# A head's query norms made chunk by chunk between the chunks of the next column block, in a linear-attention layer

## The chip, the cores and the metric

The kernel runs on one core of a Trainium2 chip. The core has five engines that run side by side, each through its own queue in order: TensorE (PE; its weight loads are shown as PEld), VectorE (DVE), ScalarE (ACT), GpSimd (POOL) and SyncE (SP), which here starts the transfers. The metric is device time in microseconds (us), the median of several runs.

## The reference, cut to what matters

The trunk has two layers over 1024 tokens behind 16 learned meta tokens, 1040 rows of width 1024, in float32. Layer A is gated DeltaNet attention with eight heads of width 128; then come a shared latent key/value set and layer B, a latent attention. The change is in layer A, where each head's queries are normalised:

```
z = h @ w_in                                        # 1040 x 4112
qkv = silu(causal_dwconv(z[..., :3072], conv_w))    # 4 taps
q, k, v = ...                                       # eight heads of 128 each
q = l2_norm(q) * (DN_DK ** -0.5)                    # x * rsqrt(sum(x*x) + EPS)
k = l2_norm(k)
...
o = gated_delta_rule(q, k, v, g, beta)              # chunkwise recurrence
o = rms_norm(o, o_gain) * silu(gate)
```

A scale on a query row only scales the output row, which is normalised again. So the kernel leaves the queries as they are and puts the sum of their squares into the epsilon of the output's norm: with s the sum of squares of a query row, the tile `epsq` holds EPS * P * s + EPS * EPS * P, and it is read once, after the last head.

## The kernel before, in words

Layer A keeps the normed input transposed in SBUF, as a high and a low part (`hT_hi`, `hT_lo`), 128 features by 1040 tokens for each of eight feature tiles. A **column block** is 128 columns of the input weight: one head's keys, values, queries or gate. `conv_acts` makes one block in three token chunks, `TOKC = [(0, 272), (272, 656), (656, 1040)]`. For each chunk `gemm_T` issues 24 matmuls on PE (eight feature tiles, three products of high and low parts, L91 to L93) into one of two "mm" banks of PSUM. ACT copies the bank to `z` (L370), POOL makes the first tap (L372), DVE the other three (L375), and ACT applies SiLU in place (shown as L82, the line of the helper `act`).

Heads go in pairs. For a pair h0, h1 the program text says: values of h0, their rows turned by PE (`natural`, L497 and L502), values of h1, queries of h0, rows of h1's values, queries of h1, `query_prep(h0)`, keys of the next pair's first head, `finish_inverses`, `query_prep(h1)`, keys of the next pair's second head, then the recurrence of both heads, step by step (`scan_tile`, L611 to L625), and the preparation of the next pair's keys. The last pair has no next keys; behind it in the text stand the gate blocks.

`query_prep` first makes the norms. ACT squares the three chunks of the head's queries `qT` into the tile `sq`. PE multiplies each of nine token tiles of `sq` (the meta tokens and eight of 128) with a column of ones, so that the sums over the 128 features fall one token to a partition (L475; a float32 matmul shows as two records, so a head has 18). DVE turns the nine columns into `epsq` with two instructions (L477). Then PE multiplies keys by queries for eight tiles (L483, 16 records) and the meta tokens (L487), and DVE multiplies by the decay (L484, L488). PSUM tiles with the tag "tr" (norms, turned rows, key by query products and more) share three banks. `sq` has the tag "vT", and with it the one buffer in which a head's values stand between `conv_acts` and `natural`.

What each engine does when is drawn up when the kernel is built: an instruction is placed on its engine's queue when, by the plan, what it needs is there, and among those that could go the earlier one in the text goes first. At run time each queue is then strictly followed, and semaphores make it wait.

Of the kernel before, what the change touches and what calls it, by code (L numbers as in the profile page):

```python
# [16 lines left out]
F32 = mybir.dt.float32  # L17
F32R = mybir.dt.float32r
BF16 = mybir.dt.bfloat16
AF = mybir.ActivationFunctionType  # L20
ALU = mybir.AluOpType
PSUM = bass.MemoryType.PSUM

P = 128
D = 1024
NM = 16
T = 1024
L = NM + T
NT = T // P
# [3 lines left out]
EPS = 1e-6  # L33
# [7 lines left out]
TOKC = [(0, 272), (272, 656), (656, 1040)]  # L41


def tok(t):

    return (0, NM) if t < 0 else (NM + P * t, NM + P * (t + 1))
# [70 lines left out]
def body(ctx: ExitStack, tc: tile.TileContext, I, out):  # L117
    nc = tc.nc
    V, A, G, TE, SY = nc.vector, nc.scalar, nc.gpsimd, nc.tensor, nc.sync
    tpool, nm, act, mm3, split_w, split_ps = tools(tc)  # L120
# [31 lines left out]
    one = ones[:, 0:1]  # L152
# [5 lines left out]
    def col(key, k=0):  # L158
        c = off[key] + k
        return pcol[:, c:c + 1]  # L160
# [21 lines left out]
    with ExitStack() as la:  # L182
# [5 lines left out]
        def bank(tag, shape):  # L188
            return pp.tile(shape, F32, tag=tag, name=nm(tag), bufs={'mm': 2, 'tr': 3, 'fin': 1, 'ch': 2}[tag])
# [17 lines left out]
        def gemm_T(hi, lo, c, m=P, tag="mm"):  # L207
            a, b = TOKC[c]
            ps = bank(tag, [P, 512])[0:m, 0:b - a]
            for kt in range(KT):  # L210
                mm3(ps, hi[:, kt, :], lo[:, kt, :], hT_hi[:, kt, a:b], hT_lo[:, kt, a:b],
                    kt == 0, kt == KT - 1)
            return ps

        with ExitStack() as l0:
# [9 lines left out]
            n = 0  # L225
# [15 lines left out]
            for c, (a, b) in enumerate(TOKC):  # L241
                tiles = [t for t in range(-1, NT) if a <= tok(t)[0] < b]
                xss = []
                for t in tiles:
# [8 lines left out]
                                    op0=ALU.mult, op1=ALU.mult)  # L253
                    xss.append((xs, r0, k))
                for kt in range(KT):
                    ps = bank("tr", [P, 512])
# [4 lines left out]
        with ExitStack() as l0:  # L261
# [8 lines left out]
            for c, (a, b) in enumerate(TOKC):  # L270
                ps = bank("fin", [P, 512])[0:4 * H, 0:b - a]
# [7 lines left out]
            ps = bank("tr", [P, 512])  # L279
            for t in range(-1, NT):  # L280
                a, b = tok(t)
                s = t if t >= 0 else NT
# [12 lines left out]
            def ntile(name, w=NT + 1):  # L295
                pool = cp if name in ("oss", "epsq", "ro", "half", "y2") else na
                return pool.tile([P, w, H], F32, tag=name, name=name)

            oss, ro = ntile("oss"), ntile("ro")
            beta, g, egc, ekd, necb, egl, epsq, nbeta = (ntile(x) for x in (  # L300
                "beta", "g", "egc", "ekd", "necb", "egl", "epsq", "nbeta"))
# [20 lines left out]
            ps = bank("tr", [P, 512])  # L322
# [17 lines left out]
        kp = ld.enter_context(tpool(name="kA", bufs=2))  # L340
# [13 lines left out]
        def weights(c0):  # L354

            n = order.index(c0)
            for c in order[n:n + 2]:
                if c not in ready:
                    ready[c] = load_w(c)
            return ready.pop(c0)  # L360

        def conv_acts(c0, tag, bufs):

            hi, lo = weights(c0)
            m = c0 // P
            z = zp.tile([P, 3 + L], F32, tag="z", name=nm("z"))
            y = kp.tile([P, L], F32, tag=tag, name=nm(tag), bufs=bufs)
            G.memset(z[:, 0:3], 0.0)
            for c, (a, b) in enumerate(TOKC):
                A.copy(z[:, 3 + a:3 + b], gemm_T(hi, lo, c))  # L370
                yc = y[:, a:b]
                G.tensor_scalar(out=yc, in0=z[:, a:b], scalar1=col("cw", m), scalar2=1.0,  # L372
                                op0=ALU.mult, op1=ALU.mult)
                for j in range(1, 4):
                    V.scalar_tensor_tensor(out=yc, in0=z[:, a + j:b + j], scalar=col("cw", 24 * j + m), in1=yc,  # L375
                                           op0=ALU.mult, op1=ALU.add)
                act(yc, yc, AF.Silu)
            return y

        def halves():  # L380
            return [(hf, slice(4 * hf, 4 * hf + 4)) for hf in range(2)]
# [83 lines left out]
        def query_prep(h, c):  # L465

            qT, kn, att, attm = c["qT"], c["kn"], c["att"], c["attm"]
            sq = kp.tile([P, L], F32, tag="vT", name=nm("sq"), bufs=1)
            ps = bank("tr", [P, 512])
            for a, b in TOKC:  # L470
                act(sq[:, a:b], qT[:, a:b], AF.Square)
            for t in range(-1, NT):
                a, b = tok(t)
                s = t if t >= 0 else NT
                TE.matmul(ps[0:b - a, s:s + 1], sq[:, a:b], one, start=True, stop=True)  # L475
            for rows, s in ((slice(0, P), slice(0, NT)), (slice(0, NM), slice(NT, NT + 1))):
                V.tensor_scalar(out=epsq[rows, s, h:h + 1].rearrange("p t o -> p (t o)"), in0=ps[rows, s],  # L477
                                scalar1=EPS * P, scalar2=EPS * EPS * P, op0=ALU.mult, op1=ALU.add)
            for half, s4 in halves():
                ps = bank("tr", [P, 512])  # L480
                for j in range(4):
                    a, b = tok(4 * half + j)
                    TE.matmul(ps[:, P * j:P * j + P], kn[:, a:b], qT[:, a:b], start=True, stop=True)  # L483
                V.tensor_tensor(out=att[half], in0=ps.rearrange("p (t i) -> p t i", i=P),  # L484
                                in1=att[half], op=ALU.mult)
            ps = bank("tr", [P, 512])
            TE.matmul(ps[:NM, 0:NM], kn[:, 0:NM], qT[:, 0:NM], start=True, stop=True)  # L487
            V.tensor_tensor(out=attm, in0=ps[:NM, 0:NM], in1=attm, op=ALU.mult)  # L488
# [103 lines left out]
        def scan_meta(h, c):  # L592
            ps = bank("ch", [P, 512])
            u = sp.tile([NM, P], F32, tag="um", name=nm("um"))
            TE.matmul(ps[:NM, 0:P], c["Nm"], c["vbm"], start=True, stop=True)
            A.copy(u, ps[:NM, 0:P])
            TE.matmul(ps[:, P:2 * P], c["kdm"], u, start=True, stop=True)
            S = sp.tile([P, P], F32, tag=f"S{h % 2}", name=nm("S"))
            V.tensor_copy(S, ps[:, P:2 * P])
            TE.matmul(ps[:NM, 2 * P:3 * P], c["attm"], u, start=True, stop=True)  # L600
            o = sp.tile([P, P], F32, tag="o", name=nm("o"), bufs=3)
            j = sp.tile([P, P], BF16, tag="js", name=nm("junk"), bufs=1)
            A.copy(o[:NM], ps[:NM, 2 * P:3 * P])
            act(j[:NM], o[:NM], AF.Square, accum_out=oss[:NM, NT, h:h + 1])
            SY.dma_start(o_scr[0:NM, h * P:(h + 1) * P], o[:NM])
            return S
# [26 lines left out]

        hs = {h: {} for h in range(H)}

        def keys_of(h):
            hs[h]["kn"] = conv_acts(D + h * P, "kn", 4)

        def values_of(h):
            hs[h]["vT"] = conv_acts(2 * D + h * P, "vT", 1)  # L640

        def queries_of(h):
            hs[h]["qT"] = conv_acts(h * P, "qT", 2)

        def value_rows(h):
            hs[h]["vb"], hs[h]["vbm"] = natural(hs[h]["vT"], beta, h, "vb")

        def prepare(h0):
            U = kp.tile([P, 2, NT, P], F32, tag="U", name=nm("U"), bufs=2)
            for h in (h0, h0 + 1):  # L650
                hs[h].update(key_prep(h, hs[h]["kn"], U[:, h - h0]))
            hs[h0]["Us"] = U
            invert_blocks((h0 // 2) % 2, h0)

        keys_of(0)
        keys_of(1)
        prepare(0)
        for h0 in range(0, H, 2):
            h1, more = h0 + 1, h0 + 2 < H
            values_of(h0)  # L660
            value_rows(h0)
            values_of(h1)
            queries_of(h0)
            value_rows(h1)
            queries_of(h1)
            query_prep(h0, hs[h0])
            if more:
                keys_of(h0 + 2)
            finish_inverses(h0, hs[h0]["Us"])
            query_prep(h1, hs[h1])  # L670
            if more:
                keys_of(h1 + 2)
            Ss = {h: scan_meta(h, hs[h]) for h in (h0, h1)}
            for t in range(NT):
                for h in (h0, h1):
                    Ss[h] = scan_tile(h, t, hs[h], Ss[h])
            if more:
                prepare(h0 + 2)
# [27 lines left out]
        norms = output_norms()  # L706
# [61 lines left out]
    def bank2(tag, shape):  # L768
        tag = {"mm": "sc", "tr": "bd", "tb": "pt"}.get(tag, tag)
        return ps_b.tile(shape, F32, tag=tag, name=nm(tag), bufs={"sc": 5, "bd": 2, "pt": 1}[tag])  # L770

    with ExitStack() as lb:
# [204 lines left out]
        with ExitStack() as lg:  # L977
            wg = lg.enter_context(tpool(name="wg", bufs=2))
            for h in range(H):
                hi, lo = wg0 if h == 0 else load_wg(wg, h)  # L980
                z = wg.tile([P, T], F32, tag="z", name=nm("z"))
                for half in range(2):
                    c = slice(512 * half, 512 * half + 512)
                    cc = slice(NM + 512 * half, NM + 512 * half + 512)
                    ps = bank2("mm", [P, 512])
# [484 lines left out]
```

## Time and profile before

| | |
|---|---|
| median of three runs | 1351.07 us |
| lowest and highest of them | 1346.55 and 1354.87 us |
| the profiled execution's own time | 1351.8 us |
| its span, from the first to the last instruction | 1350.1 us |
| granted TensorE clock, mean over the span | 0.989 |
| layer A's pairs, from the first query blocks to the last pair's recurrence | about 98 to 545 us of the span |

Times in the profile are counted from the span's start. A row of the chain of waits or of the timeline gives start, length, engine, line, operation, "out<-in" in the program's names, shapes and a count; idle time before an instruction stands in square brackets with what ended it. "tr", "mm" and so on are the tags of PSUM tiles. A row of windows gives the stretch, its width, then for each engine its busy time and instructions in brackets, then the mean granted share of the TensorE clock, the DMA engines' busy share and their GB/s.

### The profile page before, as it was taken

Reading aid. Unit: us, or ns where it says so; the run is one execution under the profiler, and the core shown is the slowest. Engines: PE = TensorE matmul, PEld = TensorE weight load, DVE = VectorE, ACT = ScalarE, POOL = GpSimd, SP = SyncE. Lnnn points to the kernel's source line nnn. Section 1 sums busy time; section 2 is a strip of 40 time slices with the busy share of each in tenths; the row PEclk is TensorE's granted clock in tenths of the full one; section 3 lists DMA queues with packets and bytes.
Section 4 is the critical chain, followed back from the end, with each engine's and each line's share of the span. In section 5 each row is a group of like instructions: output and inputs, shape, how many; then the busy total and the mean of one; then the engine's idle time right before and its main releaser. Section 6 shows DMA issues by size and latency. Waiting matters only on the chain.

```text
span 1350.1 us, 24895 instructions
## 1 busy us (share of the span) xinstructions
PE 1306.3 (97%) x9064; PEld 1181.7 (88%) x9064; DVE 900.1 (67%) x2601; ACT 534.8 (40%) x1694; POOL 412.8 (31%) x680
## 2 busy tenths in 40 slices
PE   6999999999999999999999999998999999998998
PEld 4879989989998999997888798887999999998876
DVE  6669879968978884633553765224888878788221
ACT  6442343244325322211222243116777677776100
POOL 3344224323421320060101402212535435347000
PEclk9999999999999999999999999999999999999999
DMA  6111202111211113255441302311111101014443
GB/s 185 41 25 48 56 20 62 40 42 37 59 49 32 50 32 96 72 159 178 145 147 68 95 1 84 121 47 57 44 38 35 56 21 36 21 36 149 133 124 125
DMA packets 116924, 96.81 MB, mean 72 GB/s; under 512 B 28462, under 2 KB 106094, under 8 KB 116802
## 3 DMA queue, kind: packets, MB, share of 16 engines
q1 hardware_dynamic: 116802, 95.23, 23.7%
q8 instruction: 71, 1.16, 0.4%
q14 instruction: 51, 0.42, 0.1%
HBM read 68.19 MB, written 27.01 MB: 71 GB/s over the span
## 4 chain that ended last, share of the span: by engine, by line
PE 75%; DVE 8%; DMA 5%; POOL 5%; ACT 4%; issue 3%; SPq 0%; DVEq 0%; ACTq 0%; POOLq 0%
PE mm L91 7%; PE mm L93 7%; PE mm L92 7%; PE sc L93 6%; PE sc L92 6%; PE sc L91 6%; PE bd L91 3%; PE bd L93 3%; PE bd L92 3%; PE pt L1312 2%; PE tr L483 1%; DMA raw<-in_a_w_out 1%; ACT junk L82 1%; DMA out<-raw 1%; PE ch L625 1%
## 5 line engine op out<-in xcount | busy, mean ns | idle before, releaser
L91 PE MATMUL mm<-hT_hi,whi 128*128 128x384 f32 (+1 forms) x768 | 256.8, 334 | 3.5 <-DVE whi L98 3.5
L93 PE MATMUL mm<-hT_hi,wlo 128*128 128x384 f32 (+1 forms) x768 | 255.3, 332 | 0.7 <-DVE wlo L99 0.7
L92 PE MATMUL mm<-hT_lo,whi 128*128 128x384 f32 (+1 forms) x768 | 255.7, 333 | 0.0
L91 PEld LDWEIGHTS mm<-hT_hi,whi 128*128 128x128 f32 x768 | 147.4, 192 | 5.5 <-issue 4.7
L93 PEld LDWEIGHTS mm<-hT_hi,wlo 128*128 128x128 f32 x768 | 147.5, 192 | 2.5 <-DVE wlo L99 1.3
L92 PEld LDWEIGHTS mm<-hT_lo,whi 128*128 128x128 f32 x768 | 147.2, 192 | 1.4 <-issue 0.4
L108 DVE TENSOR_TENSOR pTl<-pt,pTh 128x256 fp32r<-128x256 f32 (+2 forms) x112 | 55.0, 494 | 11.0 <-ACT pTh L107 9.5
L98 POOL TENSOR_SCALAR whi<-raw 128x512 fp32r<-128x512 f32 x48 | 37.7, 799 | 70.4 <-PE mm L92 63.8
L82 ACT ACTIVATE P<-P,mx 128x144 f32<-128x144 f32 (+3 forms) x64 | 50.6, 791 | 21.8 <-DVE mx L1270 19.0
L91 PE MATMUL sc<-wo_hi,oTh 128*128 128x512 f32 (+1 forms) x144 | 57.5, 400 | 0.6 <-issue 0.6
L93 PE MATMUL sc<-wo_hi,oTl 128*128 128x512 f32 (+1 forms) x144 | 57.2, 397 | 0.0
L92 PE MATMUL sc<-wo_lo,oTh 128*128 128x512 f32 (+1 forms) x144 | 56.9, 395 | 0.0
L375 DVE SCALAR_TENSOR_TENSOR kn<-z,pcol,kn 128x384 f32<-128x384 f32 (+1 forms) x72 | 41.4, 576 | 19.4 <-POOL kn L372 18.8
L1283 POOL TENSOR_SCALAR P<-P,sl 128x144 f32<-128x144 f32 (+3 forms) x64 | 53.0, 829 | 3.7
L370 ACT COPY z<-mm 128x384 f32<-128x384 f32 (+1 forms) x72 | 31.8, 442 | 54.4 <-PE mm L93 54.3
L107 ACT CAST pTh<-pt 128x256 fp32r<-128x256 f32 (+2 forms) x112 | 47.3, 427 | 14.1 <-PE pt L1312 8.0
L99 DVE TENSOR_TENSOR wlo<-raw,whi 128x512 fp32r<-128x512 f32 x64 | 47.1, 746 | 8.5 <-POOL whi L98 8.4
L93 PE MATMUL sc<-h_hi,wlo 128*128 128x512 f32 x128 | 50.8, 397 | 0.0
L92 PE MATMUL sc<-h_lo,whi 128*128 128x512 f32 x128 | 50.6, 396 | 0.0
L91 PE MATMUL sc<-h_hi,whi 128*128 128x512 f32 x128 | 50.5, 395 | 0.0
L91 PE MATMUL bd<-wf_hi,oTh 128*128 128x512 f32 x128 | 50.2, 392 | 0.3 <-ACT oTh L1422 0.2
L102 DVE SCALAR_TENSOR_TENSOR wlo<-raw,pcol,whi 128x128 fp32r<-128x128 f32 x64 | 23.4, 429 | 40.0 <-POOL whi L101 40.0
(380 smaller groups left out, 3951.1 us busy)
## 6 DMA issues: line engine op xcount, KB each, us to landing
raw<-in_a_w_in SPq DMA_DIRECT2D x64, 256.0 KB
xt<-in_x SPq DMA_DIRECT2D x16, 512.0 KB
o_scr<-o SPq DMA_DIRECT2D x64, 64.0 KB
raw<-in_a_w_out SPq DMA_DIRECT2D x8, 512.0 KB
on<-o_scr SPq DMA_DIRECT2D x8, 512.0 KB
x_scr<-xt SPq DMA_DIRECT2D x8, 512.0 KB
raw<-in_b_w_in SPq DMA_DIRECT2D x8, 512.0 KB
gb_scr<-z SPq DMA_DIRECT2D x8, 512.0 KB
```

Of the source, the lines that this page charges most:

```text
L82: i = A.activation(out_ap, in_ap, func, **kw)
L91: TE.matmul(ps, ahi, bhi, start=first, stop=False)
L92: TE.matmul(ps, ahi, blo, start=False, stop=False)
L93: TE.matmul(ps, alo, bhi, start=False, stop=last)
L98: eng.tensor_scalar(out=hi, in0=raw, scalar1=1.0, scalar2=1.0, op0=ALU.mult, op1=ALU.mult)
L99: V.tensor_tensor(out=lo, in0=raw, in1=hi, op=ALU.subtract)
L107: A.copy(hi, ps)
L108: V.tensor_tensor(out=lo, in0=ps, in1=hi, op=ALU.subtract)
L370: A.copy(z[:, 3 + a:3 + b], gemm_T(hi, lo, c))
L375: V.scalar_tensor_tensor(out=yc, in0=z[:, a + j:b + j], scalar=col("cw", 24 * j + m), in1=yc, op0=ALU.mult, op1=ALU.add)
L1283: G.tensor_scalar(out=Pm[:, 0:n], in0=Pm[:, 0:n], scalar1=s, scalar2=1.0, op0=ALU.mult, op1=ALU.mult)
L1312: TE.transpose(pt[:, kb, x * P:(x + 1) * P], Ps[x][0][:, y0 + kb * P:y0 + (kb + 1) * P], ident)
```

## The change

The norms leave `query_prep` and become a generator of their own, `query_norms`, which does one token chunk at each step: it squares the chunk into a scratch of 384 columns with a tag and a buffer of its own (`qsq`), takes one "tr" bank, issues the matmuls of the chunk's three 128-token tiles (the first chunk: the meta tokens and two tiles), and writes the chunk's part of `epsq` (two instructions for the first chunk, one for each other). `conv_acts` takes such a generator and advances it once behind each of its chunks. The norms of h0 are so handed to the query block of h1, and those of h1 to the key block of the next pair's first head; in the last pair, which has no such block, all three steps of h1's norms stand in a row ahead of `finish_inverses`.

```diff
-        def conv_acts(c0, tag, bufs):
+        def query_norms(h, qT):
+            for c, (a, b) in enumerate(TOKC):
+                sq = kp.tile([P, 384], F32, tag="qsq", name=nm("sq"), bufs=1)
+                act(sq[:, 0:b - a], qT[:, a:b], AF.Square)
+                ps = bank("tr", [P, 512])
+                tiles = [t for t in range(-1, NT) if a <= tok(t)[0] < b]
+                for i, t in enumerate(tiles):
+                    x, y = tok(t)
+                    TE.matmul(ps[0:y - x, i:i + 1], sq[:, x - a:y - a], one, start=True, stop=True)
+                n = tiles.count(-1)
+                for rows, s, i in ((slice(0, NM), slice(NT, NT + 1), slice(0, n)),
+                                   (slice(0, P), slice(tiles[n], tiles[-1] + 1), slice(n, len(tiles)))):
+                    if i.stop > i.start:
+                        V.tensor_scalar(out=epsq[rows, s, h:h + 1].rearrange("p t o -> p (t o)"), in0=ps[rows, i],
+                                        scalar1=EPS * P, scalar2=EPS * EPS * P, op0=ALU.mult, op1=ALU.add)
+                yield
+
+        def conv_acts(c0, tag, bufs, beside=iter(())):
...
                 act(yc, yc, AF.Silu)
+                next(beside, None)
             return y
...
         def query_prep(h, c):
             qT, kn, att, attm = c["qT"], c["kn"], c["att"], c["attm"]
-            sq = kp.tile([P, L], F32, tag="vT", name=nm("sq"), bufs=1)
-            ps = bank("tr", [P, 512])
-            for a, b in TOKC:
-                act(sq[:, a:b], qT[:, a:b], AF.Square)
-            for t in range(-1, NT):
-                a, b = tok(t)
-                s = t if t >= 0 else NT
-                TE.matmul(ps[0:b - a, s:s + 1], sq[:, a:b], one, start=True, stop=True)
-            for rows, s in ((slice(0, P), slice(0, NT)), (slice(0, NM), slice(NT, NT + 1))):
-                V.tensor_scalar(out=epsq[rows, s, h:h + 1].rearrange("p t o -> p (t o)"), in0=ps[rows, s],
-                                scalar1=EPS * P, scalar2=EPS * EPS * P, op0=ALU.mult, op1=ALU.add)
...
-            queries_of(h1)
+            queries_of(h1, query_norms(h0, hs[h0]["qT"]))
             query_prep(h0, hs[h0])
+            norms = query_norms(h1, hs[h1]["qT"])
             if more:
-                keys_of(h0 + 2)
+                keys_of(h0 + 2, norms)
+            for _ in norms:
+                pass
             finish_inverses(h0, hs[h0]["Us"])
             query_prep(h1, hs[h1])
```

(`keys_of` and `queries_of` hand the generator through.)

More of the change, by code (lines that the diff above doesn't have):

```diff
@@ L634, in body, with keys_of, queries_of @@
         hs = {h: {} for h in range(H)}
-        def keys_of(h):
-            hs[h]["kn"] = conv_acts(D + h * P, "kn", 4)
+        def keys_of(h, beside=iter(())):
+            hs[h]["kn"] = conv_acts(D + h * P, "kn", 4, beside)
         def values_of(h):
             hs[h]["vT"] = conv_acts(2 * D + h * P, "vT", 1)
-        def queries_of(h):
-            hs[h]["qT"] = conv_acts(h * P, "qT", 2)
+        def queries_of(h, beside=iter(())):
+            hs[h]["qT"] = conv_acts(h * P, "qT", 2, beside)
         def value_rows(h):
```

## The prediction

> **What bounds the kernel now.** I read the head of the page first.
>
> ```profile
> PE 1306.3 (97%) x9064; PEld 1181.7 (88%) x9064; DVE 900.1 (67%) x2601; ACT 534.8 (40%) x1694; POOL 412.8 (31%) x680
> ```
>
> TensorE is busy 97% of the span, far ahead of VectorE with 67%. The page's line of the granted clock shows the same tenth in every slice, but a slice is a fortieth of the span, some 34 us, so a dip of a few us hides in it. Next I asked for the stretch that the change touches, from the first query block to the end of the last pair's preparation (columns: width, then busy us and instructions of PE, PEld, DVE, ACT, POOL, then granted clock, DMA share, GB/s).
>
> ```profile
> 98.00:545.00 447.00, 444.67 (x3697) 417.10 (x3697) 367.94 (x1044) 144.52 (x479) 135.49 (x197) 0.98 0.19 48
> ```
>
> Here PE is idle 2.33 us out of 447, so hardly a wait is left to remove; what TensorE has to do, and how fast its clock runs, sets the end. The mean clock of 0.98 is the thing to chase: 2% of 447 us. The chain of waits shows where the time differs.
>
> ```profile
> 126.41 2.01 PE tr L475 x18
> 128.42 3.52 PE tr L483 x16
> ...
> 145.77 1.89 PE tr L483 x16
> ```
>
> The same 16 matmuls of L483 took 3.52 us after one head's norms and 1.89 us after another's. So I cut the windows of L475 (the norm's one-column matmuls) along the edges of the slow stretches, which are 3.41 us wide (columns: width, busy us and records of PE, then of PEld, granted clock, DMA share, GB/s; L475 alone, but the clock is the window's).
>
> ```profile
> 124.97:128.38 3.41, 2.04 (x18) 1.97 (x18) 1.00 0.24 69
> 128.38:131.79 3.41, 0.04 (x1) 0.00 (x0) 0.50 0.00 0
> 142.03:145.45 3.42, 1.76 (x17) 1.74 (x17) 1.00 0.00 0
> 145.45:148.86 3.41, 0.32 (x3) 0.23 (x3) 1.00 0.20 50
> 244.43:247.85 3.42, 1.15 (x11) 1.13 (x12) 1.00 0.43 116
> 247.85:251.26 3.41, 0.93 (x9) 0.84 (x8) 1.00 0.00 0
> 261.50:264.91 3.41, 2.08 (x18) 1.97 (x18) 1.00 0.00 0
> 264.91:268.33 3.42, 0.00 (x0) 0.00 (x0) 0.50 0.25 62
> ...
> 490.19:493.61 3.42, 1.70 (x16) 1.61 (x15) 1.00 0.01 2
> 493.61:497.02 3.41, 0.00 (x0) 0.00 (x0) 1.00 0.00 0
> 497.02:500.43 3.41, 2.08 (x18) 1.97 (x18) 1.00 0.00 0
> 500.43:503.85 3.42, 0.00 (x0) 0.00 (x0) 0.50 0.00 0
> ```
>
> Each pair of rows is one head's norms and the window behind them; the two pairs left out, from 367.31 and from 384.38 us, read as the one from 261.50 does, so all eight heads are told here. Five times a head's 18 records fall whole into one window (PEld 1.97 us), and each time the next window runs at 0.50. Three times an edge cuts them (1.74 at most on one side), and the next window keeps 1.00. So a solid run of one-column matmuls seems to count as idleness for the clock, and the limit lies between 1.74 and 1.97 us in one window. L483 does not count so:
>
> ```profile
> 491.75 2.03 PE L483 MATMUL tr<-qT,kn 128*128 128x128 f32 x16
> ```
>
> From there to its end the window 490.19:493.61 holds L483 alone, behind 1.61 us of L475, and the clock stays.
>
> **The change part by part.**
>
> *The run is cut.* A head's nine norm matmuls (18 records, 2.01 us) become three of 6 records, 6 x 2.01/18 = 0.67 us each, with a chunk of 24 matmuls of the next column block between. Those 24 start 0.13 us apart for 272 columns and 0.175 us apart for 384 (rows below), so 3 to 4.2 us lie between two groups, and no window can hold more than about 0.67 us, or 1.3 us when two groups sit at its ends. Both are below 1.74, so the five half-clock windows should go. The price of one: the 16 matmuls of L483 lose 3.52 - 1.89 = 1.63 us when they fill it; a 272-column matmul starts every 0.22 us in it against 0.13 us outside.
>
> ```profile
> 125.90 0.34 PE L92 MATMUL mm<-hT_lo,whi 128*128 128x384 f32 x1
> 126.07 0.34 PE L93 MATMUL mm<-hT_hi,wlo 128*128 128x384 f32 x1
> 126.34 0.40 PE L475 MATMUL tr<-ones,sq 128*16 128x1 f32 x3
> ...
> 250.77 0.39 PE L91 MATMUL mm<-hT_hi,whi 128*128 128x272 f32 x1
> 251.00 0.29 PE L92 MATMUL mm<-hT_lo,whi 128*128 128x272 f32 x1
> 251.13 0.29 PE L93 MATMUL mm<-hT_hi,wlo 128*128 128x272 f32 x1
> ...
> 373.17 0.43 PE L91 MATMUL mm<-hT_hi,whi 128*128 128x272 f32 x1
> 373.39 0.43 PE L92 MATMUL mm<-hT_lo,whi 128*128 128x272 f32 x1
> ```
>
> That is 41 to 47% of 3.41 us, 1.4 to 1.63 us; at most half, 1.71 us. I take 1.55 us, nearest to the L483 pair. Five of them: **-7.8 us** (bounds -7.0 and -8.5).
>
> *More islands.* The step into the norms costs TensorE a little: 126.07 to 126.34 is 0.27 us where 125.90 to 126.07 is 0.17, so 0.09 to 0.10 us. The step back too: 250.77, the first block matmul after a head's L487, to 251.00 is 0.23 us where 251.00 to 251.13 is 0.13, another 0.10 us. Before, norms and L483 of a head make one island. Now a pair's first head has its first two chunks alone (the third still runs into its L483), two islands more; its second head has three more. Four pairs x 5 x 0.19 us = **+3.8 us**. If the weights of a small group are loaded in time, the step in is free: bound +2.0 us; if each group waits for its weights as long as the whole gap of 0.27 us, +7.4 us.
>
> *Squares and scratch.* The 24 Square instructions (eight heads by three chunks) stay 24, on the same slices, on an engine that is busy 144.52 of 447 us. Before, they borrowed the value block's buffer, and so began late: the first two start at 115.28, just after the last read of that buffer at 114.65.
>
> ```profile
> 114.65 0.27 PE L502 MATMUL tr<-ident,vT 128*16 128x128 f32 x1
> ...
> 115.28 0.84 ACT L82 ACTIVATE sq<-qT 128x272 f32<-128x272 f32 x2
> 120.16 0.53 ACT L82 ACTIVATE qT<-qT 128x384 f32<-128x384 f32 x1 [4.03 <-DVE qT L375]
> ```
>
> PE did not wait for them, so an earlier start gains nothing. The new scratch has one buffer, so a chunk's Square waits for the chunk before it to be read; behind it on ACT stand the copies that empty the block's PSUM banks. The cover is the 3 to 4.2 us of block matmuls between two groups, against 0.67 us for the group and 0.42 us for a Square (0.84 us for two): cost 0. Without that cover it would be those 0.42 us at each of 24 chunks, 10 us.
>
> *Epsilon and banks.* A head has four of the small VectorE instructions instead of two, 16 more at 148 ns, 2.4 us. VectorE is busy 367.94 of 447 us, mostly with work that runs beside PE; I put 0.6 us on the path (bounds 0 and 2.4). Each chunk takes one of three "tr" banks; the one wait seen there was this.
>
> ```profile
> PE tr L487 <- DVE epsq L477: 0.8, 1, 0.8
> ...
> L477 DVE TENSOR_SCALAR epsq<-tr x16: 138/148/177, 130.8 to 499.9; 128x8 f32<-128x8 f32 x8, 16x1 f32<-16x1 f32 x8
> ```
>
> With the readings spread it may go, or come back at another bank: between -0.8 and +0.8; I take **-0.8 us**. No DMA and nothing on SyncE's or GpSimd's queue is added or moved. When PE is faster, VectorE is late next: it was busy 82% here.
>
> **Sum:** -7.8 + 3.8 + 0.6 - 0.8 = -4.2 us. Against the profiled execution's own 1351.8 us that is **1347.6 us**. The median of the runs shown is 1351.07, 0.7 us less; that they spread over 8.3 us fits a free number of slow windows, as an edge may or may not cut a run.
>
> The Trainium skill, "TensorE: Matmul & The Clock Gate" (Part 1: The HAM clock gate), says that the clock is judged in a free-running window of about 3.4 us and halves after an idle one. Window and ratio agree with the 3.41 us and 0.50 above. But its advice speaks only of PE idle for a whole window, which no window above was. By its wording norms cannot be the cause, and cutting them saves nothing; that is the first rival.
>
> **The rivals.**
>
> *The half clock has another cause.* If it is a matter of time or load, the five windows come back elsewhere and only the islands and VectorE's instructions remain: 1351.8 + 3.8 + 0.6 = 1356.2 us. For it: other slow windows exist outside this stretch. Against: eight of eight heads sort cleanly by 1.74 and 1.97 us.
>
> *The norms stay together.* Each engine's order is planned from readiness as well as from the text: the Squares at 115.28 went ahead of an earlier line's Silu at 120.16. Were the three groups gathered again, nothing changes: 1351 to 1353 us. Against: norms now follow each chunk in the text and their input is ready early.
>
> *PE stalls between chunks (slower).* TensorE's queue is in order. If a chunk's Square stands on ACT behind the Silu of the block being computed, PE reaches the norms first and waits.
>
> ```profile
> ACT qT L82 <- DVE qT L375: 65.1, 24, 4.0
> ```
>
> ACT waits 65.1/24 = 2.7 us for such a Silu. At 24 places that is 65 us, 1413 us; it decides for the worse from two places on, and with six, 1347.6 + 16 = 1364 us. Against it stands the order at 115.28 again.
>
> *Better than forecast:* islands at their lower bound, and some slow windows outside this stretch missed by luck: about 1343 us or less.
>
> **How the numbers follow.** Forecast 0.60 (1345 to 1351), another cause 0.11, together 0.10, stalls 0.08, better 0.11. The range of 1341 to 1357 us leaves out the stalls and the far end of the better case. One per cent, 13.5 us, is about what a measurement here can tell from no change. Faster by over 1% (below 1337.6) needs more than all five windows and no islands: 0.05. Slower by over 1% (above 1364.6) needs six or more stalls: 0.06. Within: 0.89.
>
> **What would show it.** In the changed profile: no 0.50 window in the stretch after a query norm; norm matmuls in groups of 6 with block matmuls between; first and second matmul after each group 0.1 us late; L483 at 1.9 us for all heads; PE idle there still under 4 us. Wrong would be: half-clock windows as many as before, or PE waiting for ACT at the norms' line.

## The result and the profile after

The changed kernel takes 1354.21 us (median of 20 runs, 1349.49 to 1362.4), the kernel before 1351.74 us (20 runs, 1346.55 to 1355.18): a ratio of 1.0031, 95% interval 1.002 to 1.0041. It is a little slower, where a little faster had been forecast: 1347.6 us. Ratios here and below are taken over fast runs, and the one slow run of them all (1376.09 us, of the last experiment) is left out of its numbers. The profiled execution after took 1355.2 us, with a span of 1353.5 us.

First the stretch of layer A's pairs and the clock (the row of windows as before: width, PE, PEld, DVE, ACT, POOL, then granted clock).

```profile
98.00:545.00 447.00, 437.92 (x3684) 411.13 (x3683) 362.17 (x1051) 147.56 (x477) 129.18 (x197) 0.99 0.19 47
```

Two things moved against each other. The clock here rose from 0.98 to 0.99: two half-clock windows are left in this stretch where there were five. But TensorE, which had been idle for 2.33 us, is now idle for 447.00 - 437.92 = 9.08 us. The chain of waits shows that the norms are cut as meant: groups of 6, and L483 (now L492) at 1.89 us behind six of the eight heads.

```profile
242.96 0.67 PE tr L371 x6
253.37 1.89 PE tr L492 x16
258.62 0.67 PE tr L371 x6
269.03 1.89 PE tr L492 x16
```

The list of who waited for whom (total us, times, longest) names the new idleness, and the timeline shows where it begins.

```profile
PE tr L371 <- DVE vb L507: 5.7, 3, 2.7
```

```profile
114.74 1.03 PE L506 MATMUL tr<-ident,vT 128*128 128x128 f32 x8
...
115.61 0.27 PE L511 MATMUL tr<-ident,vT 128*16 128x128 f32 x1
...
122.14 0.74 PE L371 MATMUL tr<-ones,sq 128*16 128x1 f32 x6 [2.69 <-DVE vb L507]
...
121.41 0.68 DVE L507 TENSOR_TENSOR vb<-tr,beta 128x512 f32<-128x512 f32 x1
122.01 0.39 DVE L533 TENSOR_TENSOR tmp<-M 66x231 f32<-66x231 f32 x1
122.31 0.68 DVE L507 TENSOR_TENSOR vb<-tr,beta 128x512 f32<-128x512 f32 x1
122.92 0.39 DVE L536 TENSOR_TENSOR M<-M,tmp 66x231 f32<-66x231 f32 x1
123.22 0.33 DVE L512 TENSOR_SCALAR vbm<-tr,beta 16x128 f32<-16x128 f32 x1
```

Read it from the top. At 114.74 to 115.88 us PE turns the second head's value rows and so fills all three "tr" banks. The first norm group of the other head needs one of them and is due one chunk of block matmuls later, at 122.14 - 2.69 = 119.45. VectorE, in order and busy with convolutions and the block inversion, empties the first bank only at 121.41 + 0.68 = 122.09. PE's queue is in order too, so everything stands still. The same happens in the third and fourth pair (1.89 and 1.14 us). And the clock falls behind the stall as it fell behind the one-column run:

```profile
120.30:123.71 3.41, 1.57 (x12) 1.55 (x13) 3.41 (x10) 1.32 (x3) 0.74 (x2) 1.00 0.21 64
123.71:127.12 3.41, 3.41 (x12) 3.41 (x12) 3.41 (x12) 0.00 (x0) 0.00 (x0) 0.50 0.29 77
```

In the first of these windows PE is idle for 3.41 - 1.57 = 1.84 us and has the norm group for another 0.74 us; what each of the two contributes is not separated. The other half-clock window of the stretch, from 294.38 us, stands behind no norm: the window before it holds 92 matmuls of 32 by 32 of the block inversion (L580, L582), with PE idle for 0.71 us.

The difference of the two profiled spans, 3.4 us, is not all the change's. The last record in front of it already stands 0.96 us later (L502 at 114.65 before, L511 at 115.61 after). From there to the gate blocks the new kernel loses another 1.4 us (the same block matmul starts at 109.56 and 110.52 us, later one at 583.09 and 585.46): 6.7 us more idleness and about 4.8 us less lost in half-clock windows (the distance from each record to the next against the same pair of records at full clock: about 8.0 us in five windows before, 3.2 us in two after). What is left, the islands among it, is then about -0.5 us, so nothing remains that the islands would have cost. About 1 us more is lost behind that, where the gate weights are late in both; that was not looked into.

The profiled pair flatters the clock. Every run has its mean granted clock, and a half-clock window costs half of 3.41 us of it, so (1 - clock) x span / 1.707 counts the windows of a run, those outside this stretch too. The kernel before has 0.9888 over 62 runs with a mean span of 1349.7 us, 8.9 windows; the changed one 0.9899 over 20 runs with 1353.4 us, 8.0. On average the change saves about one window and not three.

### The profile page after: what moved, and what is told of

It reads as the page before. It is cut to its first block, busy times and chain, and to the rows that moved or that the text cites. A ratio compares the mean times of both kernels' runs of the same rounds, so it can differ in the third digit from the quotient of the medians.

```text
span 1353.5 us, 24948 instructions
## 1 busy us (share of the span) xinstructions
PE 1301.6 (96%) x9064; PEld 1178.7 (87%) x9064; DVE 896.4 (66%) x2617; ACT 537.2 (40%) x1694; POOL 404.4 (30%) x680
## 4 chain that ended last, share of the span: by engine, by line
PE 76%; DVE 7%; issue 5%; POOL 5%; ACT 3%; DMA 3%; SPq 0%; DVEq 0%; POOLq 0%; ACTq 0%
PE mm L91 7%; PE mm L93 7%; PE mm L92 7%; PE sc L93 6%; PE sc L92 6%; PE sc L91 6%; PE bd L91 5%; PE bd L93 4%; PE bd L92 4%; PE pt L1324 2%; PE po L93 1%; PE tr L492 1%; PE po L92 1%; PE tr L371 1%; PE sc L1277 1%
## 5 line engine op out<-in xcount | busy, mean ns | idle before, releaser
L98 POOL TENSOR_SCALAR whi<-raw 128x512 fp32r<-128x512 f32 x48 | 34.7, 739 | 78.3 <-PE mm L92 71.8
L1295 POOL TENSOR_SCALAR P<-P,sl 128x144 f32<-128x144 f32 (+3 forms) x64 | 50.1, 784 | 3.7
L1293 POOL TENSOR_SCALAR Pe<-P,sl 128x128 f32<-128x128 f32 x64 | 29.5, 462 | 71.2 <-DVE sl L1290 51.9
```

The source lines that it names most:

```text
L98: eng.tensor_scalar(out=hi, in0=raw, scalar1=1.0, scalar2=1.0, op0=ALU.mult, op1=ALU.mult)
L1293: G.tensor_scalar(out=Pe, in0=Pm[:, None, 0:NM].broadcast_to([P, E8, NM]), scalar1=s, scalar2=1.0, op0=ALU.mult, op1=ALU.mult)
L1295: G.tensor_scalar(out=Pm[:, 0:n], in0=Pm[:, 0:n], scalar1=s, scalar2=1.0, op0=ALU.mult, op1=ALU.mult)
```

## The experiments

All times are medians, each beside runs of the kernel before on the same chip; the ratio is to those, with its 95% interval.

**Another bank.** In `query_norms`:

```diff
-                ps = bank("tr", [P, 512])
+                ps = bank("fin", [P, 512])
```

> The changed kernel with the norms' sums in the bank tagged fin, which no query or key block uses, in place of one of the three tr banks. Bank theory: the 2.69, 1.89 and 1.14 us in which TensorE waited for VectorE's vb at the first norm chunk of a pair are the wait for a tr bank; they go, the half-clock window behind the longest goes too, and the time falls by 5.7 us for the stalls and about 1.6 us for the window, to some 1347 us, 4 us under the kernel before. Rival (the single scratch buffer or the islands cost the time): the waits stay at the same place under another name, or go with no gain, and the time stays at 1353 to 1355 us.

1349.6 us, ratio 1.000 (0.9984 to 1.0015): level with the kernel before, and not the gain expected. The wait for vb is gone, but there is one fin bank, each chunk takes it anew, and in each pair the second chunk of the first head must wait until VectorE has read the first:

```profile
PE fin L371 <- DVE epsq L376: 3.9, 4, 1.8
```

**128 columns of ones in the kernel before.**

```diff
-            for t in range(-1, NT):
+            for t in (*range(NT), -1):
...
-                TE.matmul(ps[0:b - a, s:s + 1], sq[:, a:b], one, start=True, stop=True)
+                TE.matmul(ps[0:b - a, s:s + P], sq[:, a:b], ones, start=True, stop=True)
```

> The kernel before, norms still in one run of 18 records, but each multiplies by 128 columns of ones in place of one (the sums are the same; a later tile overwrites the surplus columns). Clock theory: one-column matmuls count as idleness; a 128-column float32 matmul starts every 0.112 us too (L483), so TensorE's work stays the same, the half-clock windows behind the norms go, and the time falls by four to five windows of 1.55 us, 6 to 8 us, to about 1345 us. Rival (the windows come by time or load, or any small float32 matmul brings them): as many half-clock windows behind the norms as before, 1350 to 1353 us.

1378.18 us, ratio 1.0197 (1.0178 to 1.0216). The time went the other way, but the part on the clock held. These are the windows that contain a head's whole run, with the window behind (L475 alone; the clock is the window's):

```profile
125.09:128.50 3.41, 2.19 (x18) 2.04 (x18) 1.00 0.24 67
128.50:131.92 3.42, 0.07 (x1) 0.00 (x0) 1.00 0.00 0
258.21:261.62 3.41, 2.27 (x18) 2.04 (x18) 1.00 0.24 67
261.62:265.04 3.42, 0.00 (x0) 0.00 (x0) 1.00 0.00 0
384.51:387.92 3.41, 2.27 (x18) 2.04 (x18) 1.00 0.49 143
387.92:391.33 3.41, 0.00 (x0) 0.00 (x0) 1.00 0.00 0
514.21:517.62 3.41, 2.27 (x18) 2.04 (x18) 1.00 0.23 65
517.62:521.04 3.42, 0.00 (x0) 0.00 (x0) 1.00 0.00 0
```

The same count of records, whole in one window; with one column the next window was at half clock five times of five, with 128 columns none of four. What cost the time is an order: in this build the epsilon readings stand later on VectorE's queue, and L487 needs their bank.

```profile
PE tr L487 <- DVE epsq L477: 20.5, 7, 4.6
```

The stretch has eight half-clock windows all the same: four behind these waits, and four in a row from 172.88 us behind the block inversion and a wait of 1.5 us.

**The scratch alone.** In `query_prep` of the kernel before, one bank and two readings as there, but

```diff
+            for c0, c1 in TOKC:
+                sq = kp.tile([P, 384], F32, tag="qsq", name=nm("sq"), bufs=1)
+                act(sq[:, 0:c1 - c0], qT[:, c0:c1], AF.Square)
+                ... # the chunk's matmuls
```

> One part of the change alone: the norms stay in one place in front of a head's key by query products and in one tr bank, but go chunk by chunk through the new scratch of 384 columns with one buffer. Bank theory: no stall of over 1 us at the norms, as nothing asks for a tr bank earlier than before; the time is that of the kernel before or, if the groups of 6 come apart on TensorE, up to 6 us less through fewer half-clock windows: 1345 to 1352 us. Rival (the single buffer costs the time): 1353 us or more, with TensorE or ACT waiting for the scratch.

1363.46 us, ratio 1.0079 (1.0058 to 1.0101): the rival. With nothing planned between the chunks, PE waits once a pair, at the second group of the first head, for a Square that waits for the scratch.

```profile
PE tr L476 <- ACT sq L82: 8.1, 4, 2.7
```

**The first head's norms one chunk later.**

```diff
-            queries_of(h1, query_norms(h0, hs[h0]["qT"]))
+            late = query_norms(h0, hs[h0]["qT"])
+            queries_of(h1, chain((None,), late))
+            for _ in late:
+                pass
```

> The changed kernel with the first head's norms begun one chunk later: first chunk behind the second chunk of the query block, second behind the third, third right after it. Bank theory: VectorE then has 4 us more to read vb out of the three tr banks, so the stall at the first norm chunk shrinks from 1.1 to 2.7 us to under 0.5 us, the half-clock window behind it goes, and the time is 1347 to 1349 us. Rival (the cost is elsewhere): stall or time unchanged, 1353 to 1355 us.

1353.64 us, ratio 1.0011 (0.9997 to 1.0026). The wait for vb is gone, as the bank theory said. But the third chunk now follows the second with no block matmuls between, and the scratch takes its place, so the time is not what was expected:

```profile
PE tr L371 <- ACT sq L82: 4.4, 3, 2.6
```

**One fin bank a head, squares in the values' buffer.** The norms stay where the change put them; the bank is taken once, and all nine sums are read after the third chunk.

```diff
         def query_norms(h, qT):
+            ps = bank("fin", [P, 512])
+            sq = kp.tile([P, L], F32, tag="vT", name=nm("sq"), bufs=1)
             for c, (a, b) in enumerate(TOKC):
...
+                if c == len(TOKC) - 1:
+                    ... # two tensor_scalar, as before the change
                 yield
```

> The changed kernel with the norms at the new place, but the squares in the values' buffer as before the change (1040 columns, no chunk waits for another) and all nine sums of a head in one fin bank, read by two VectorE instructions after the third chunk. Theory (the place is right, the two waits cost the gain: for a bank still to be read by VectorE, and for the one scratch buffer): no stall over 0.5 us at the norms, no half-clock window between the first query block and the gate blocks, 1344 to 1347 us, below the kernel before (1352). Rival (the islands or the place itself cost the time): 1350 us or more with no stall at the norms.

1347.7 us, ratio 0.9969 (0.9953 to 0.9985): faster than both kernels. One expectation failed: a half-clock window is left in the stretch, from 493.72 us, behind the norms of the last head.

**128 columns in the kernel before, fin bank.** As the second experiment, with `bank("fin", ...)`.

> The kernel before with the norms in one run at the old place, each multiplying by 128 columns of ones as in e2_wide, but the sums in the fin bank, so that the meta tokens' product (L487) need not wait for VectorE's late epsilon. Clock theory: with that stall gone no half-clock window is left at the norms and the time falls by some four windows of 1.6 us, to 1344 to 1347 us. Rival (the windows in the kernel before come from VectorE's lateness and not from the one-column run): half-clock windows right behind the norms stay and 1350 us or more.

1358.99 us, ratio 1.0058 (1.0038 to 1.0077). Again the time missed and the clock part held. Seven heads' runs are cut by an edge here; one lies whole in a window, and the clock stays:

```profile
174.87:178.28 3.41, 2.29 (x18) 1.97 (x18) 1.00 0.02 5
178.28:181.70 3.42, 0.00 (x0) 0.00 (x0) 1.00 0.00 0
```

The plan moved other work again, and PE waits elsewhere; three half-clock windows of the stretch stand behind such waits and none behind norms:

```profile
PE mm L91 <- ACT z L370: 4.1, 3, 2.6
PE fin L566 <- DMA T<-blk_out: 3.9, 3, 1.8
PE tr L483 <- DVE att L484: 2.2, 1, 2.2
```

**One fin bank a head, with the change's scratch.** As the fifth, with `sq` in the `qsq` tag of 384 columns, one buffer.

> As e5_vT_fin, but with the change's scratch of 384 columns and one buffer. If the single buffer costs time at the new place too, TensorE waits for the Square at the second or third chunk, 0.5 to 2 us a pair, and the time is 2 to 5 us over e5_vT_fin. If the cover of a whole chunk of block matmuls is enough, as the prediction had it, the two are within 1 us.

1346.91 us, ratio 0.9966 (0.9949 to 0.9983), within 1 us of the fifth: at the new place the single scratch costs nothing that shows. With the fifth, from which it cannot be told apart, it is the fastest version of the study. Its stretch and two of its waits:

```profile
98.00:545.00 447.00, 445.12 (x3741) 417.77 (x3740) 372.35 (x1059) 147.05 (x486) 134.50 (x197) 1.00 0.19 48
```

```profile
PE fin L372 <- DVE epsq L375: 0.5, 1, 0.5
PE ch L603 <- DVE ksc L420: 0.5, 1, 0.5
```

TensorE is idle for 1.88 us and the clock reads 1.00: nearly the state that the prediction described. The profiled execution, 1342.96 us, is the fastest of the nine; by the count above the nine have 6.6 half-clock windows a run against 9.0 for the kernel before on that chip. The 2.4 windows fewer, at about 1.6 us each, are 3.8 of the 4.6 us gained.

One half-clock window is left in the stretch, and it is the one-column run again. The last pair's second head has no key block to stand in, so its three groups of 6 fall within 3.6 us, and 16 records share a window (L372 alone):

```profile
490.82:494.23 3.41, 2.04 (x16) 1.78 (x15) 1.00 0.00 0
494.23:497.64 3.41, 0.00 (x0) 0.00 (x0) 0.50 0.00 0
```

**Each norm matmul twice, in the kernel before.**

```diff
+                TE.matmul(ps[0:b - a, 16 + s:17 + s], sq[:, a:b], one, start=True, stop=True)
                 TE.matmul(ps[0:b - a, s:s + 1], sq[:, a:b], one, start=True, stop=True)
```

> The kernel before with each norm matmul made twice, the second time into columns that nobody reads: 36 records a head in one run of 4 us. 144 records more at 0.112 us are 16 us. Clock theory: a run of 4 us always fills some window with more than 1.7 us, so all eight heads have a half-clock window behind their norms, some two: 4 to 12 windows more than before at 1.6 us, 6 to 19 us, in all 1374 to 1387 us. Rival (windows come by time or load): five or fewer windows there, 1366 to 1370 us.

1375.75 us, ratio 1.0182 (1.0148 to 1.0215). The median is in the range, but no run is near it: three took 1369 to 1371 us, below the range, and three 1381 us, inside it. The profile is of one of the lower three, and the windows in it are what tells for the theory: all eight heads have half-clock windows behind them, eleven in the stretch against five.

```profile
98.00:545.00 447.00, 445.64 (x3576) 422.44 (x3575) 357.26 (x1014) 138.00 (x457) 132.44 (x196) 0.96 0.18 45
```

PE is as busy as ever, and the clock fell to 0.96.

**One bank a head, but a tr bank.** The one difference from the seventh is the tag.

> As e7_scratch_fin, but the one bank of a head's sums is again one of the three tr banks: the changed kernel with one bank and one reading a head in place of three. If the wait for a tr bank that VectorE has yet to empty is the cost, it stays at the first norm chunk (1 to 3 us a pair) and the time is 1351 to 1355 us. Rival (three banks and readings a head are the cost, whatever their tag): as e7_scratch_fin, 1346 to 1348 us.

1356.99 us, ratio 1.0052 (1.0034 to 1.007). The wait is back, with two half-clock windows behind the longest stall:

```profile
PE tr L372 <- DVE vb L506: 3.0, 1, 3.0
PE tr L372 <- DVE att L492: 1.8, 2, 1.1
```

Not all of the loss is the bank's: six more half-clock windows of the stretch come in two rows of three, from 501.56 us around the norms of the last head and from 539.10 us behind the block inversion.

**The fin bank in the kernel before.** One word changed in `query_prep`.

> The kernel before with nothing changed but the tag of the norms' bank, fin in place of tr. If e7_scratch_fin gains by the cut run and not by the bank, half-clock windows still stand behind the norms wherever a window holds the whole run, and the time is that of the kernel before, 1350 to 1353 us. Rival (a relieved tr bank is the gain): 1346 to 1348 us.

1354.99 us, ratio 1.0036 (1.0015 to 1.0057). There is no gain, so a relieved tr bank alone is not what the seventh gains by. That it is slower than the kernel before was not expected, and the clock accounts for it: by the count above its eleven runs have 13.3 half-clock windows each against 9.0 on that chip, and 4.3 windows at about 1.6 us are more than the 4.6 us between the two means. The profile has six in the stretch against five. The one run of norms that lies whole in a window is followed by half clock once more:

```profile
126.67:130.09 3.42, 2.08 (x18) 1.97 (x18) 1.00 0.07 19
130.09:133.50 3.41, 0.00 (x0) 0.00 (x0) 0.50 0.00 0
```

But another window falls to half clock with no norm before it (all engines' work now: width, PE, PEld, DVE, ACT, POOL, then granted clock):

```profile
171.05:174.46 3.41, 3.41 (x43) 2.75 (x42) 1.29 (x2) 0.91 (x3) 1.68 (x4) 1.00 0.03 7
174.46:177.87 3.41, 3.41 (x19) 3.19 (x19) 1.97 (x5) 0.00 (x0) 0.77 (x2) 0.50 0.00 0
```

PE is busy throughout the first of them, and 32 of its 43 records are matmuls of 64 by 64 of the block inversion (L581). The other four half-clock windows, two each from 300.75 and 423.63 us, stand behind such matmuls mixed with norms, which this plan put there. So a window without norms and without idleness can bring the half clock too; that the small matmuls did it is likely, but was not tested.

## Why the prediction was wrong, point by point

**The clock: the mechanism right and shown, the number not.** One-column runs bring the half clock: with 128 columns it went (none of five whole runs), with the run doubled it came behind every head. The price was 1.55 us a window in the prediction and about 8.0/5 = 1.6 us by the records. But five windows could not be counted on. The sum took all eight heads as cut by a chunk of 24 matmuls, and the last pair's second head, which is one of the five, is not. In the changed kernel an edge happens to cut its groups (15 records in one window, and the clock stays); in the fifth and seventh experiment it does not, and the half clock comes. Two new windows came in the changed kernel's stretch besides, one of them behind the stall. The limit of 1.74 to 1.97 us is not sharp either: 1.78 us brought the half clock in the seventh, 1.81 us did not in the tenth (491.90 to 495.31 us); the other work in the windows differed.

**Epsilon and banks: the step that failed.** It stood at -0.8 us, with +0.8 as its worst; in the changed kernel the idleness of the stretch grew by 6.7 us, 5.7 us of it in three waits of the norms for a bank. The prediction named the three banks and then looked at the one wait that the trace of before had. It did not ask who would still hold the banks at the new place. That trace could have told: VectorE reads there the turned value rows in 120.34 to 122.60 us,

```profile
120.34 0.68 DVE L498 TENSOR_TENSOR vb<-tr,beta 128x512 f32<-128x512 f32 x1
121.25 0.68 DVE L498 TENSOR_TENSOR vb<-tr,beta 128x512 f32<-128x512 f32 x1
122.27 0.33 DVE L503 TENSOR_SCALAR vbm<-tr,beta 16x128 f32<-16x128 f32 x1
```

which is 6 us after PE wrote them at 114 us. At 126.34 us the old norms came behind that; the new first group, due at 119.45 - 0.96 = 118.49 us by that trace's clock, comes ahead of it, and the first bank is free only at 120.34 + 0.68 = 121.02 us. A wait of about 2.5 us was there to be worked out; 2.69 us was measured. The four kernels that cross tag and number of banks bear it out, each as a ratio to the kernel before: tr, three a head (the change) 1.0031; tr, one 1.0052; fin, three 1.000; fin, one 0.9966. Both are needed: a bank that is not being read, and no reading between the chunks.

**The slower rival: right in kind, wrong in its cause.** It had PE reach the norms too early and stand still in order, which is what happened, but behind VectorE and the banks and not behind ACT's Square, and at three places of 24.

**Islands: too dear.** +3.8 us was forecast, and the balance above leaves nothing for them. The step into most groups costs nothing (247.62 to 247.79 us is a block matmul's normal distance), the step back 0.07 us (248.38 to 248.63, against 0.18), and there are only nine more stretches of other work between block matmuls than before (229 against 220), where the forecast counted twenty: groups fell together with other work.

```profile
247.62 0.34 PE L93 MATMUL mm<-hT_hi,wlo 128*128 128x384 f32 x1
247.79 0.72 PE L371 MATMUL tr<-ones,sq 128*128 128x1 f32 x6
248.38 0.42 PE L91 MATMUL mm<-hT_hi,whi 128*128 128x384 f32 x1
248.63 0.33 PE L92 MATMUL mm<-hT_lo,whi 128*128 128x384 f32 x1
```

**Scratch and cover: right.** With a chunk of block matmuls between the groups it costs nothing (the seventh against the fifth); without them it cost 0.8% (the third).

**The half clock without idleness.** The Trainium skill, "TensorE: Matmul & The Clock Gate" (Part 1: The HAM clock gate), has the clock halve after an idle window. The runs differ in what counts as one: 1.97 us of one-column matmuls in 3.41 us was enough while PE was busy throughout, and so, in the changed kernel, was a window with 1.84 us of idleness and the first group behind it, not a whole idle window. So the rival drawn from its wording, that cutting the run saves nothing, fell with the fifth and seventh experiment.

## What to carry to other kernels

A moved step takes its resources at the new time: for each bank it asks for, look up in the old trace when the last reader there finishes, not only which waits exist. A dense engine's clock is a resource too; a run of tiny matmuls that shows as 100% busy can put the next 3.4 us at half clock, and cutting it paid here only where the cut made no new stall. And a plan drawn up by readiness shifts with every edit, so a one-word change has to be measured.

## What was not expected of the hardware

Records of a float32 matmul with one column and with 128 columns start nearly equally far apart, about 0.112 and 0.118 us (18 records in 2.01 us; 16 of L483 in 1.89 us; the expectations took 0.112 us for both), but only behind the first did the clock fall. So nine tiny matmuls in a row are paid for twice where one window holds them all: in their own 2 us, and by whatever runs in the 3.4 us behind them. A window mostly of 64 by 64 matmuls, with no norm in it, brought the half clock too (the tenth experiment).
